# A wait behind one cast, and the order of the last stores, in a convolution with max pooling

## The chip, the core and the metric

The kernel runs on one core of one Trainium2 chip. The metric is the device time of one execution in microseconds (us): 105.42 us is the median of three runs before the change (105.28, 105.42 and 109.23). The core has five engines that each work through a queue of their own in order and wait for each other by semaphores: TensorE (PE, matmuls; PEld are its weight loads), VectorE (DVE), ScalarE (ACT), GpSimd (POOL), and SyncE (SP), which here only issues DMA transfers. Sixteen DMA engines move data between the device's memory and the on-chip memory.

## The reference

A 3x3 convolution without bias over 16 images of 64 channels and 64x64 pixels, to 128 channels, zero-padded by one pixel, then a 2x2 maximum without overlap. Input, weights and output are float32; the output is 16x128x32x32.

```python
x_pad = np.pad(x, ((0, 0), (0, 0), (pad, pad), (pad, pad)), mode='constant')
for b ...: for co ...: for ci ...: for kh ...: for kw ...:
    conv[b, co] += weight[co, ci, kh, kw] * x_pad[b, ci, kh:kh+h, kw:kw+w]
for b ...: for c ...: for i ...: for j ...:
    output[b, c, i, j] = np.max(conv[b, c, i*2:(i+1)*2, j*2:(j+1)*2])
```

## The kernel before

**Steps.** Two images are handled together: the 64 channels of the first lie on partitions 0 to 63, those of the second on 64 to 127. Each of the 8 pairs is cut into four quarters of 16 input rows, which gives 32 steps; a step makes 8 rows by 32 columns of pooled output for each of its two images. In the names, `24.1` is step 24 and its second image. An accumulator bank holds 8 rows by 64 columns of convolution for 128 output channels; there are eight banks.

**Two ways to compute a step.** Pooling needs two convolution rows at a time, y0 and y1, from four input rows x(-1), x0, x1, x2. With G0, G1, G2 the three kernel rows (each three taps, one matmul per tap, on 64 rows of partitions), a step of kind K takes the sum x0 + x1 (`KS`) on VectorE, multiplies it by G1 for both rows (`PR`), and makes two partial sums A (`PAa`, `PAb`) and B (`PBa`, `PBb`) from weights that are differences (D2 = G2 - G1, D0 = G0 - G1). A step of kind W makes S = x0 + x1, E = x0 - x1 and V, the differences of rows two apart, and has four products: `P2` (E), `P0` and `P3` (V), `P1` (S). In both the part common to y0 and y1 is added after the maximum of A and B.

**Around the products.** For each image of a step, ScalarE copies A out (`EV`) and, for kind W, copies A after `P2` into B's bank (`SE`, the seed); for some steps it also lifts a set of input rows into a bank (`CP`). VectorE takes the maximum of the two rows (`MX`). ScalarE copies the odd columns out (`OD`), and VectorE takes the maximum of even and odd columns into the output tile (`CM`). The very last image has its maximum over column pairs in one operation, in two halves (`RM`). `ST` stores a step's output tile of 256 KB; steps 30 and 31 are stored image by image (128 KB), the last image in halves of 64 KB, and the very last half is issued by ScalarE, all others by SyncE.

**Inputs.** W steps read float32 rows from the tiles `wx` (`LX`, issued by SyncE). K steps read bfloat16 rows from `kx`, which a GpSimd DMA casts on its way (`LK`), but for the first two K steps (0 and 2): these come as float32 into `kf` (`LX.0a`, `LX.0b`, `LX.2`) and are cast by an engine, `XO` for odd rows and `XE` for even ones. `XO.0a` (first half of step 0) is given to VectorE, the other four casts to ScalarE. A load waits (`paced`) for the column maxima of the step 12 or 13 places earlier.

**What sets the order.** The text ORDER is written out by hand as it stands: tokens in the order in which the program is recorded. Each engine gets its own tokens in that order, and nothing reorders them. A token on one engine does not hold back a token on another; only semaphores do, and they follow from the data, from the reuse of buffers and from one hand-made rule. A store thus waits for its step's `CM`, and whatever stands behind it on SyncE waits with it.

**The hand-made rule** is in `row_op` (line 194 is its operation): an element-wise row operation on GpSimd also waits for the last row operation that was recorded for VectorE before it, which `last_row` holds. VectorE's operations that read a bank beside the rows (line 288), its casts (line 189) and its work on banks are not held in it.

**The head around the change**, by engine, from the tokens: VectorE has V.1, TV.GP (line 240), XO.0a (line 189), TV.D0 and TV.G1 (line 242), E.3 and S.3 (line 288), then the row maxima of step 1. GpSimd has S.1, V.3, two casting loads (LK.5, LK.9), then S.4. TensorE has P0.1 for both images (its data named wv), then the first PAa of step 0 (kx), P3.1 (wv), more of step 0 (kx), P2.3 (we), again step 0, P1.1 (ws) and P0.3 (wv). ScalarE has SE.1, XO.0b and XE.0a, CP.3 (line 284), EV.1 twice, XE.0b and XE.2, EV.0 twice, SE.3 twice (line 421).

**The tail around the change**: behind the last load, SyncE's queue holds the stores of steps 21, 18, 22, 17, 15, 14, 16, 20, 26, 19, 23, 24, 28, 27, 25, 29, then 30.1, 30.0, 31.0 and the first half of 31.1.

Of the kernel before, what the change touches and what calls it, by code (L numbers as in the profile page):

```python
# [61 lines left out]
MX.22.0 P1.22.0 P3.24.1 CM.21.1 CM.20.1 LX.29 S.25:v SE.24.0:1 EV.24.1 OD.22.0 KS.27:v PAa.23.1:4  # L62
P2.25.0:2 E.26:g CM.22.0 ST.13 MX.24.1 P0.24.0 P2.25.1:7 SE.25.0:5 EV.24.0 PAb.23.1 P3.24.0 P0.25.0
PBa.23.1:6 MX.24.0 P1.24.1 PBa.23.0:0 KS.23:v EV.23.1 EV.25.0 SE.25.1:4 V.26:v LX.31 OD.24.1 S.26:g
LX.30 P1.24.0 PBb.23.1 OD.24.0 V.28:g E.29:g P3.25.0 P2.26.1:2 CM.24.1 ST.21 ST.18 SE.26.1:3 S.29:g
P0.25.1 PBb.23.0 CM.24.0 ST.22 ST.17 EV.25.1 P2.26.0:1 P3.25.1 SE.26.0:7 MX.25.0 MX.23.0 V.29:g
E.31:g P0.26.1 P1.25.0 MX.25.1 MX.23.1 OD.25.0 V.30:g ST.15 P3.26.1 PR.23.0 EV.26.1 OD.23.0 P0.26.0
P1.25.1 EV.26.0 CM.25.0 P3.26.0 PR.23.1 PAa.27.0:2 PAa.27.1:5 MX.26.1 CM.23.0 CP.28:1 ST.14 MX.26.0
OD.23.1 P1.26.1 PBa.27.0:0 OD.25.1 E.28:v CM.25.1 PAb.27.0 PAb.27.1 V.31:g PBb.27.0 P2.28.1:4
OD.26.1 ST.16 EV.27.0 CM.26.1 P1.26.0 PBa.27.1:3 CM.23.1 EV.27.1 P2.29.0:6 PBb.27.1 SE.28.1:2 S.28:v  # L70
OD.26.0 MX.27.0 CP.30:5 CM.26.0 PR.27.0 P0.28.1 SE.29.0:1 MX.27.1 OD.27.0 P3.28.1 P2.28.0:7 EV.28.1
E.30:v CM.27.0 P0.29.0 PR.27.1 SE.28.0:4 EV.29.0 OD.27.1 P3.29.0 P2.29.1:0 MX.28.1 ST.20 P1.28.1
P0.28.0 ST.26 ST.19 S.30:v ST.23 SE.29.1:6 P3.28.0 P2.30.1:5 MX.29.0 EV.28.0 OD.28.1 CM.27.1 P1.29.0
P0.29.1 SE.30.1:7 MX.28.0 S.31:g P2.30.0:3 P3.29.1 EV.29.1 CM.28.1 ST.24 P0.30.1 P1.28.0 OD.29.0
P3.30.1 P2.31.0:2 SE.30.0:0 EV.30.1 OD.28.0 CM.29.0 MX.29.1 MX.30.1 CM.28.0 P2.31.1:1 P0.30.0
SE.31.0:5 EV.30.0 P3.30.0 P1.29.1 P0.31.0 P1.30.1 SE.31.1:4 OD.29.1 MX.30.0 P0.31.1 P3.31.0 EV.31.0
CM.29.1 MX.31.0 EV.31.1 P3.31.1 P1.30.0 MX.31.1 P1.31.0 OD.30.1 OD.30.0 CM.30.1 ST.28 ST.27 ST.25
ST.29 ST.30.1 CM.30.0 ST.30.0 OD.31.0 P1.31.1 CM.31.0 RM.31.1a RM.31.1b ST.31.0 ST.31.1a ST.31.1b:a
"""


# [1 line left out]
def kernel(  # L83
# [98 lines left out]

    eng = {"v": nc.vector, "a": nc.scalar, "g": nc.gpsimd}

    def cast(e, out, in_):
        if e == "a":
            nc.scalar.copy(out=out, in_=in_)
        else:
            eng[e].tensor_copy(out=out, in_=in_)  # L189

    last_row = [None]

    def row_op(e, out, in0, in1, op):
        inst = eng[e].tensor_tensor(out=out, in0=in0, in1=in1, op=op)  # L194
# [5 lines left out]
    def weights(m, e):  # L200
        if m in ("g0", "g1", "g2"):
            cast(e, slots(m.upper()), {"g0": g0, "g1": g1, "g2": g2}[m])
        elif m == "D2":
            row_op(e, slots("D2"), g2, g1, SUB)
        elif m == "D0":
            row_op(e, slots("D0"), g0, g1, SUB)
        elif m == "GS":
            row_op(e, gsum, wv[:, 0:3, :], wv[:, 6:9, :], ADD)
        elif m == "GM":
            row_op(e, slots("GM"), ring(gsum, 0), g1, SUB)  # L210
        elif m == "GP":
            row_op(e, slots("GP"), ring(gsum, 0), g1, ADD)
# [58 lines left out]
    def to_bf16(s, part, odd, e):  # L271
        p, lo, hi = chunk(s)
        a, b = {"": (lo, hi), "a": (lo, half(s)), "b": (half(s), hi)}[part]
        a += (a % 2) != odd
        cast(e, kx_of(p)[:, a:b:2, :], kf[s][:, a - lo : b - lo : 2, :])
# [42 lines left out]
    def rs_cast(s, e):  # L318
        t = row["S", s] = row_pool.tile([128, R, W], BF16, name="ws")
        cast(e, t, wrow(s, 0))  # L320
# [263 lines left out]
```

## Time and profile before

| | |
|---|---|
| median of three runs | 105.42 us |
| the profiled execution | 104.88 us |
| its span, first to last instruction | 103.1 us |
| granted TensorE clock, mean | 0.998 |
| DMA over the span | 24.07 MB, 233 GB/s |

In the rows of a timeline the columns are the start in us from the beginning of the span, the length in us, the engine, the line, the operation, output and input by the program's names with partitions by elements and type, and how many instructions are merged (x2). In brackets stands how long the engine had been idle before, and what released it. Rows of a wait name the waiting engine and its line, then what it waited for: the total in us, how often, and the longest. Rows of DMA issues give the issuing queue, the size and the time from issue to landing. PEld rows are weight loads, which run ahead of the matmuls that use them. The ends of matmuls are modelled; their starts are what to go by.

### The profile page before, as it was taken

Reading aid. Unit: us, or ns where it says so; the run is one execution under the profiler, and the core shown is the slowest. Engines: PE = TensorE matmul, PEld = TensorE weight load, DVE = VectorE, ACT = ScalarE, POOL = GpSimd, SP = SyncE. Lnnn points to the kernel's source line nnn. Section 1 sums busy time; section 2 is a strip of 40 time slices with the busy share of each in tenths; the row PEclk is TensorE's granted clock in tenths of the full one; section 3 lists DMA queues with packets and bytes.
Section 4 is the critical chain, followed back from the end, with each engine's and each line's share of the span. In section 5 each row is a group of like instructions: output and inputs, shape, how many; then the busy total and the mean of one; then the engine's idle time right before and its main releaser. Section 6 shows DMA issues by size and latency. Waiting matters only on the chain.

```text
span 103.1 us, 2478 instructions
## 1 busy us (share of the span) xinstructions
PE 95.7 (93%) x870; PEld 51.9 (50%) x870; DVE 91.0 (88%) x176; ACT 89.4 (87%) x199; POOL 80.8 (78%) x63
## 2 busy tenths in 40 slices
PE   6696999999999999999999999999999999999920
PEld 2153754555555567565555575555444446455300
DVE  1599899999989999999999999778989999978860
ACT  4596999887989999998899999999998989999810
POOL 5006978999599969999998999999962999997000
PEclk9999999999999999999999999999999999999999
DMA  2989999839940699999999972898669700740881
GB/s 62 307 241 416 418 417 325 178 96 352 257 130 11 159 221 332 256 302 269 272 390 375 385 283 56 233 256 240 247 226 339 254 6 0 239 168 0 288 276 56
DMA packets 13789, 24.07 MB, mean 233 GB/s; under 512 B 1104, under 2 KB 9680, under 8 KB 13776
## 3 DMA queue, kind: packets, MB, share of 16 engines
q1 hardware_dynamic: 12768, 22.29, 64.5%
q0 software_dynamic: 864, 1.56, 8.5%
q8 instruction: 7, 0.11, 0.4%
q10 hardware_dynamic: 144, 0.07, 0.2%
q14 instruction: 6, 0.05, 0.2%
HBM read 17.07 MB, written 8.39 MB: 247 GB/s over the span
## 4 chain that ended last, share of the span: by engine, by line
PE 82%; DVE 7%; DMA 3%; ACT 3%; issue 1%; DVEq 0%; ACTq 0%
PE acc L393 82%; DMA wraw<-in_weight_dram 3%; DVE wq L194 2%; DVE kx L189 1%; ACT ev L408 1%; DVE wv L194 1%; DVE acc L425 1%; DVE we L194 1%; ACT od L448 1%; DVE gsum L194 0%; ACT acc L284 0%; ACT acc L421 0%; DVE o L457 0%; DVE wt L240 0%; DVEq L579 0%
## 5 line engine op out<-in xcount | busy, mean ns | idle before, releaser
L393 PEld LDWEIGHTS <-wt 64*128 64x128 bf16 x840 | 49.6, 94 | 41.4 <-issue 3.7
L393 PE MATMUL acc<-wv,wt 64*128 64x504 bf16 (+1 forms) x288 | 63.4, 377 | 0.5 <-DVE wt L240 0.5
L194 POOL TENSOR_TENSOR wv<-wx 128x1024 bf16<-128x1024 f32 x21 | 49.3, 2362 | 1.5 <-DMA wx<-in_x_dram 0.6
L425 DVE TENSOR_TENSOR acc<-acc,ev 128x512 f32<-128x512 f32 x64 | 43.6, 692 | 2.7 <-ACT ev L408 1.4
L393 PE MATMUL acc<-kx,wt 64*128 64x504 bf16 (+6 forms) x216 | 38.4, 350 | 0.4 <-DVE kx L189 0.4
L393 PE MATMUL acc<-we,wt 64*128 64x512 bf16 (+1 forms) x144 | 36.8, 376 | 0.1
L393 PE MATMUL acc<-ws,wt 64*128 64x512 bf16 (+1 forms) x144 | 35.0, 377 | 0.2 <-DVE acc L425 0.2
L408 ACT ACTIVATE ev<-acc 128x512 f32<-128x512 f32 x48 | 28.8, 605 | 1.5 <-PE acc L393 1.2
L421 ACT COPY acc<-acc 128x512 f32<-128x512 f32 x48 | 28.2, 591 | 1.3 <-DVE o L457 0.4
L457 DVE TENSOR_TENSOR o<-acc,od 128x256 f32<-128x256 f32 x63 | 25.0, 416 | 1.8 <-ACT od L448 1.3
L448 ACT COPY od<-acc 128x256 f32<-128x256 f32 x63 | 22.8, 379 | 1.6 <-PE acc L393 1.2
L194 POOL TENSOR_TENSOR ws<-wx 128x512 bf16<-128x512 f32 x12 | 15.2, 1273 | 9.6 <-DVE wv L194 6.2
L194 POOL TENSOR_TENSOR we<-wx 128x512 bf16<-128x512 f32 x10 | 12.7, 1272 | 2.0 <-DVE ks L194 1.2
L393 PE MATMUL acc<-ks,wt 64*128 64x504 bf16 (+1 forms) x48 | 12.9, 376 | 0.0
L410 ACT COPY ev<-acc 128x512 f32<-128x512 f32 x16 | 9.3, 595 | 1.0 <-PE acc L393 0.8
L288 DVE TENSOR_TENSOR we<-acc,wx 128x512 bf16<-128x512 f32 x11 | 7.5, 683 | 0.7 <-ACT acc L284 0.5
L288 DVE TENSOR_TENSOR ws<-acc,wx 128x512 bf16<-128x512 f32 x11 | 7.5, 679 | 0.0
L284 ACT COPY acc<-wx 128x512 f32<-128x512 f32 x11 | 6.7, 607 | 0.6 <-DMA wx<-in_x_dram 0.6
L485 PE MATMUL acc<-const-bfloat16-1.0 128*128 128x512 bf16 x8 | 3.3, 595 | 0.8 <-PEq L565 0.8
L194 DVE TENSOR_TENSOR ks<-kx 128x512 bf16<-128x512 bf16 x8 | 4.0, 511 | 0.0
L194 DVE TENSOR_TENSOR wv<-wx 128x1024 bf16<-128x1024 f32 x3 | 3.7, 1217 | 0.0
L269 POOL DMA_DIRECT2D kx<-in_x_dram x6 | 3.5, 586 | 0.0
(28 smaller groups left out, 23.0 us busy)
## 6 DMA issues: line engine op xcount, KB each, us to landing
out_dram<-o SPq DMA_DIRECT2D x30, 256.0 KB, 4.3
wx<-in_x_dram SPq DMA_DIRECT2D x12, 512.0 KB, 7.3
wx<-in_x_dram SPq DMA_DIRECT2D x6, 544.0 KB, 5.2
wx<-in_x_dram SPq DMA_DIRECT2D x6, 480.0 KB, 7.9
kx<-in_x_dram POOLq DMA_DIRECT2D x3, 256.0 KB, 7.8
kf<-in_x_dram SPq DMA_DIRECT2D x1, 512.0 KB, 8.2
kx<-in_x_dram POOLq DMA_DIRECT2D x2, 240.0 KB, 8.0
out_dram<-o SPq DMA_DIRECT2D x3, 128.0 KB, 2.9
```

Source lines behind the costliest of these rows:

```text
L194: inst = eng[e].tensor_tensor(out=out, in0=in0, in1=in1, op=op)
L269: paced(s, nc.gpsimd.dma_start(out=kx_of(p)[:, lo:hi, :], in_=rows_of(p, lo, hi)))
L284: nc.scalar.copy(out=acc[bank], in_=wrow(s, 0))
L288: nc.vector.tensor_tensor(out=t, in0=lifted[s], in1=wrow(s, 1), op=op)
L393: yield lambda kw=kw, o0=o0, o1=o1, c0=c0, c1=c1: nc.tensor.matmul(acc[t][:, i0:i1, o0:o1], wt[l * CI : l * CI + CI, K * BLOCKS[block] + T ...
L408: inst = nc.scalar.mul(t, acc[bank["A", s, l]], -1.0)
L410: inst = nc.scalar.copy(out=t, in_=acc[bank["A", s, l]])
L421: nc.scalar.copy(out=acc[b], in_=acc[bank["A", s, l]])
L425: nc.vector.tensor_tensor(out=t, in0=t, in1=ev[s, l], op=MAX)
L448: nc.scalar.copy(out=od[s, l][:, i0:i1], in_=acc[bank["B", s, l]][:, i0:i1, 1::2])
L457: done[s, l] = nc.vector.tensor_tensor(out=outs(s)[:, l, i0:i1], in0=acc[bank["B", s, l]][:, i0:i1, 0::2], in1=od[s, l][:, i0:i1], op=MAX,)
L485: nc.tensor.matmul(acc[n], ones[:, 0:128], ones, start=True, stop=True, skip_group_check=True)
```

## The change

First, `cast` records its operation in `last_row` when it runs on VectorE or GpSimd, so that GpSimd row operations recorded behind it wait for it too. Second, in the text ORDER the stores behind the last load (LX.30) are moved: each stands right behind the last `CM` of its step, those of steps already finished directly behind the load; ST.31.0 stands ahead of the last two `RM`. SyncE's queue behind the last load becomes 21, 18, 22, 17, 15, 14, 16, 20, 19, 24, 25, 23, 26, 27, 28, 29, 30.1, 30.0, 31.0 and the first half of 31.1. No instruction is added or taken away, and the queues of the other engines keep their order.

```diff
-LX.30 P1.24.0 PBb.23.1 OD.24.0 V.28:g E.29:g P3.25.0 P2.26.1:2 CM.24.1 ST.21 ST.18 SE.26.1:3 S.29:g
...
+LX.30 ST.21 ST.18 ST.22 ST.17 ST.15 ST.14 ST.16 ST.20 ST.19 P1.24.0 PBb.23.1 OD.24.0 V.28:g E.29:g
+P3.25.0 P2.26.1:2 CM.24.1 SE.26.1:3 S.29:g P0.25.1 PBb.23.0 CM.24.0 ST.24 EV.25.1 P2.26.0:1 P3.25.1
...
+MX.26.1 CM.23.0 CP.28:1 MX.26.0 OD.23.1 P1.26.1 PBa.27.0:0 OD.25.1 E.28:v CM.25.1 ST.25 PAb.27.0
+PAb.27.1 V.31:g PBb.27.0 P2.28.1:4 OD.26.1 EV.27.0 CM.26.1 P1.26.0 PBa.27.1:3 CM.23.1 ST.23 EV.27.1
+P2.29.0:6 PBb.27.1 SE.28.1:2 S.28:v OD.26.0 MX.27.0 CP.30:5 CM.26.0 ST.26 PR.27.0 P0.28.1 SE.29.0:1
...
+CM.27.1 ST.27 P1.29.0 P0.29.1 SE.30.1:7 MX.28.0 S.31:g P2.30.0:3 P3.29.1 EV.29.1 CM.28.1 P0.30.1
+P1.28.0 OD.29.0 P3.30.1 P2.31.0:2 SE.30.0:0 EV.30.1 OD.28.0 CM.29.0 MX.29.1 MX.30.1 CM.28.0 ST.28
...
+P0.31.1 P3.31.0 EV.31.0 CM.29.1 ST.29 MX.31.0 EV.31.1 P3.31.1 P1.30.0 MX.31.1 P1.31.0 OD.30.1
+OD.30.0 CM.30.1 ST.30.1 CM.30.0 ST.30.0 OD.31.0 P1.31.1 CM.31.0 ST.31.0 RM.31.1a ST.31.1a RM.31.1b
+ST.31.1b:a

+    last_row = [None]
+
     def cast(e, out, in_):
         if e == "a":
             nc.scalar.copy(out=out, in_=in_)
         else:
-            eng[e].tensor_copy(out=out, in_=in_)
-
-    last_row = [None]
+            last_row[0] = eng[e].tensor_copy(out=out, in_=in_)
```

More of the change, by code (lines that the diff above doesn't have):

```diff
@@ L64 @@
 PBa.23.1:6 MX.24.0 P1.24.1 PBa.23.0:0 KS.23:v EV.23.1 EV.25.0 SE.25.1:4 V.26:v LX.31 OD.24.1 S.26:g
-LX.30 P1.24.0 PBb.23.1 OD.24.0 V.28:g E.29:g P3.25.0 P2.26.1:2 CM.24.1 ST.21 ST.18 SE.26.1:3 S.29:g
-P0.25.1 PBb.23.0 CM.24.0 ST.22 ST.17 EV.25.1 P2.26.0:1 P3.25.1 SE.26.0:7 MX.25.0 MX.23.0 V.29:g
-E.31:g P0.26.1 P1.25.0 MX.25.1 MX.23.1 OD.25.0 V.30:g ST.15 P3.26.1 PR.23.0 EV.26.1 OD.23.0 P0.26.0
-P1.25.1 EV.26.0 CM.25.0 P3.26.0 PR.23.1 PAa.27.0:2 PAa.27.1:5 MX.26.1 CM.23.0 CP.28:1 ST.14 MX.26.0
@@ L69 @@
[L69 to L78, printed above, removed]
+LX.30 ST.21 ST.18 ST.22 ST.17 ST.15 ST.14 ST.16 ST.20 ST.19 P1.24.0 PBb.23.1 OD.24.0 V.28:g E.29:g
+P3.25.0 P2.26.1:2 CM.24.1 SE.26.1:3 S.29:g P0.25.1 PBb.23.0 CM.24.0 ST.24 EV.25.1 P2.26.0:1 P3.25.1
@@ new lines @@
+SE.26.0:7 MX.25.0 MX.23.0 V.29:g E.31:g P0.26.1 P1.25.0 MX.25.1 MX.23.1 OD.25.0 V.30:g P3.26.1
+PR.23.0 EV.26.1 OD.23.0 P0.26.0 P1.25.1 EV.26.0 CM.25.0 P3.26.0 PR.23.1 PAa.27.0:2 PAa.27.1:5
+MX.26.1 CM.23.0 CP.28:1 MX.26.0 OD.23.1 P1.26.1 PBa.27.0:0 OD.25.1 E.28:v CM.25.1 ST.25 PAb.27.0
+PAb.27.1 V.31:g PBb.27.0 P2.28.1:4 OD.26.1 EV.27.0 CM.26.1 P1.26.0 PBa.27.1:3 CM.23.1 ST.23 EV.27.1
+P2.29.0:6 PBb.27.1 SE.28.1:2 S.28:v OD.26.0 MX.27.0 CP.30:5 CM.26.0 ST.26 PR.27.0 P0.28.1 SE.29.0:1
+MX.27.1 OD.27.0 P3.28.1 P2.28.0:7 EV.28.1 E.30:v CM.27.0 P0.29.0 PR.27.1 SE.28.0:4 EV.29.0 OD.27.1
@@ new lines @@
+P3.29.0 P2.29.1:0 MX.28.1 P1.28.1 P0.28.0 S.30:v SE.29.1:6 P3.28.0 P2.30.1:5 MX.29.0 EV.28.0 OD.28.1
+CM.27.1 ST.27 P1.29.0 P0.29.1 SE.30.1:7 MX.28.0 S.31:g P2.30.0:3 P3.29.1 EV.29.1 CM.28.1 P0.30.1
+P1.28.0 OD.29.0 P3.30.1 P2.31.0:2 SE.30.0:0 EV.30.1 OD.28.0 CM.29.0 MX.29.1 MX.30.1 CM.28.0 ST.28
+P2.31.1:1 P0.30.0 SE.31.0:5 EV.30.0 P3.30.0 P1.29.1 P0.31.0 P1.30.1 SE.31.1:4 OD.29.1 MX.30.0
+P0.31.1 P3.31.0 EV.31.0 CM.29.1 ST.29 MX.31.0 EV.31.1 P3.31.1 P1.30.0 MX.31.1 P1.31.0 OD.30.1
+OD.30.0 CM.30.1 ST.30.1 CM.30.0 ST.30.0 OD.31.0 P1.31.1 CM.31.0 ST.31.0 RM.31.1a ST.31.1a RM.31.1b
```

## The prediction

> **What bounds the kernel now.** First the page's busy times and the chain that ended last, then the pieces of that chain in order of time (start, length, what).
>
> ```profile
> PE 95.7 (93%) x870; PEld 51.9 (50%) x870; DVE 91.0 (88%) x176; ACT 89.4 (87%) x199; POOL 80.8 (78%) x63
> ...
> PE 82%; DVE 7%; DMA 3%; ACT 3%; issue 1%; DVEq 0%; ACTq 0%
> ```
>
> ```profile
> 9.65 35.60 PE acc L393 x346
> ...
> 47.85 48.56 PE acc L393 x442
> ...
> 99.28 0.33 DVE o L467
> ```
>
> From 9.65 to 96.4 us TensorE runs from matmul to matmul, but for 2.6 us around 45 to 48. Four engines are near full, so a gain at one place lasts only if no other engine sets the pace right behind it. The two edits touch the two ends: the head before 9.65 us, and the last stores.
>
> **Part 1, the wait.** In the order, the one cast given to VectorE is XO.0a; the next GpSimd operations behind it are S.1 and V.3, and S.1, being first, carries the wait. No other GpSimd operation is affected: the next row operation of VectorE (KS.0) takes over as what is waited for. The timeline of the head, by engine:
>
> ```profile
> 8.37 1.23 DVE L189 CAST kx<-kf 128x256 bf16<-128x256 f32 x1
> 9.52 0.61 DVE L242 COPY wt<-acc 128x384 bf16<-128x384 bf16 x2
> ```
>
> ```profile
> 8.19 1.26 POOL L194 TENSOR_TENSOR ws<-wx 128x512 bf16<-128x512 f32 x1 [6.22 <-DVE wv L194]
> 10.02 2.37 POOL L194 TENSOR_TENSOR wv<-wx 128x1024 bf16<-128x1024 f32 x1 [0.56 <-DMA wx<-in_x_dram]
> ```
>
> ```profile
> 8.46 0.82 PE L393 MATMUL acc<-wv,wt 64*128 64x512 bf16 x6 [0.49 <-DVE wt L240]
> 9.65 0.51 PE L393 MATMUL acc<-kx,wt 64*128 64x256 bf16 x6 [0.37 <-DVE kx L189]
> ...
> 13.50 0.82 PE L393 MATMUL acc<-ws,wt 64*128 64x512 bf16 x6
> 14.15 1.14 PE L393 MATMUL acc<-wv,wt 64*128 64x512 bf16 x7
> ```
>
> The cast begins 0.18 us into S.1 (8.19 to 9.45) and ends at 9.60, 0.15 us after it: it looks held by S.1. TensorE waits for it. What the cast takes alone is not in the trace. Below, 0.15 us, what was left of it behind S.1; above, 1.23 us, if it is slow by itself. The nearest row of its size is this one of VectorE:
>
> ```profile
> L457 DVE TENSOR_TENSOR o<-acc,od 128x256 f32<-128x256 f32 x63 | 25.0, 416 | 1.8 <-ACT od L448 1.3
> ```
>
> I take 0.3 us, under those 416 ns. Then the cast ends at 8.67. TensorE is free at 8.46 + 0.65 = 9.11 (six such matmuls take 0.65 from start to start, 13.50 to 14.15), so it starts its cast rows at 9.11 and not at 9.65: 0.54 us earlier. At 1.23 us nothing is won here.
>
> The Trainium skill, "SBUF — State Buffer", section "SBUF: two separate sides", has a rule for this: a VectorE operation in a two-port mode and a GpSimd operation exclude each other, and the later one is blocked until the first has ended. By that rule the cast is short alone; the two rows above agree (0.15 us behind the end at 9.45). By it the sum of this part would be as I take it, 0.54 us at TensorE's start.
>
> The added wait costs GpSimd: S.1 starts at 8.67 + 0.09 (the handover seen before it, from wv's end at 8.10 to 8.19) = 8.76 and ends at 10.02, 0.57 later. Behind it in the queue stands V.3, which sat 0.56 us idle for its load until 10.02 anyway, so the load hides it. With the upper bound S.1 runs from 9.69 to 10.95, V.3 ends at 13.32 in place of 12.39, and its reader, the wv matmuls at 14.15, still does not wait. Lost on GpSimd: nothing in both cases. The two copies of VectorE behind the cast come earlier, beside S.1; held by it they would start near 10.0, 0.5 us later than now, and end at 10.6, before VectorE's next work, which waits for ScalarE.
>
> What is late next? ScalarE, whose rows behind the head are these, and with them TensorE's weight loads:
>
> ```profile
> 10.05 0.59 ACT L284 COPY acc<-wx 128x512 f32<-128x512 f32 x1 [0.56 <-DMA wx<-in_x_dram]
> 10.58 1.08 ACT L408 ACTIVATE ev<-acc 128x512 f32<-128x512 f32 x2
> 11.54 0.93 ACT L187 CAST kx<-kf 128x256 bf16<-128x256 f32 x2
> 12.36 1.08 ACT L410 COPY ev<-acc 128x512 f32<-128x512 f32 x2
> 13.31 1.10 ACT L421 COPY acc<-acc 128x512 f32<-128x512 f32 x2
> ```
>
> ```profile
> 13.98 0.10 PEld L393 LDWEIGHTS <-wt 64*128 64x128 bf16 x2 [0.15 <-ACT acc L421]
> 14.46 0.54 PEld L393 LDWEIGHTS <-wt 64*128 64x128 bf16 x7 [0.39 <-issue]
> ```
>
> ScalarE is released at 10.02 by a load that the change does not touch, and from 10.05 to 14.41 it has no gap. Its last two copies, the seeds of step 3 (SE.3.0 to 13.90, SE.3.1 to 14.41), release TensorE's P0.3 products: the weight loads resume at 13.98 and 14.46, 0.05 to 0.08 us behind each copy. TensorE coming 0.54 us earlier stands there and waits. So I count the head's 0.54 us as lost again by 14.46: sum of part 1, **0.0 us**; the ends are 0 and 0.54 won.
>
> **Part 2, the stores.** SyncE issues in order, and a store waits for its step's column maximum on VectorE. No load moves: the order up to LX.30 is kept, and the eight stores behind it are the same in both (21, 18, 22, 17, 15, 14, 16, 20), so the loads' company is as before. SyncE's issues and its wait, before (of the last row's eight, the first is ST.28, then 27, 25, 29 and the four that hold steps 30 and 31):
>
> ```profile
> 79.04 0.71 SPq L480 DMA_DIRECT2D out_dram<-o  x1
> ```
>
> ```profile
> SPq L480 <- DVE o L457: 7.7, 1, 7.7
> ```
>
> ```profile
> 87.48 1.97 SPq L480 DMA_DIRECT2D out_dram<-o  x4
> ```
>
> ```profile
> 94.87 5.09 SPq L480 DMA_DIRECT2D out_dram<-o  x8
> ```
>
> After the store at 79.04 (ST.20), ST.26 blocks the queue for 7.7 us; ST.19, 23 and 24, long done, stand behind it. Then ST.28 blocks ST.27 and ST.25 until 94.87. The stretches of 2 us show the cost (last two columns: DMA share, GB/s):
>
> ```profile
> 84.00:86.00 2.00, 2.00 (x23) 1.15 (x19) 1.99 (x5) 1.57 (x5) 2.00 (x2) 1.00 0.00 0
> ...
> 92.00:94.00 2.00, 2.00 (x22) 1.06 (x19) 1.45 (x4) 2.00 (x6) 2.00 (x2) 1.00 0.00 0
> ...
> 96.00:98.00 2.00, 1.77 (x14) 0.63 (x11) 1.76 (x4) 1.44 (x4) 0.00 (x0) 1.00 1.04 341
> 98.00:100.00 2.00, 0.66 (x4) 0.09 (x1) 1.54 (x5) 0.37 (x1) 0.00 (x0) 1.00 0.83 278
> ```
>
> The DMA engines idle and are then full for the last 4 us. After the change ST.19 goes out behind ST.20, and 24, 25, 23, 26, 27 each at its step, so of the group at 94.87 only ST.28 and ST.29 are left before the last ones: 512 KB fewer. No waiter on VectorE's buffers shows in the stretch; earlier stores only free them earlier. ST.26 goes from first to fifth of these, and still has over 10 us to the end.
>
> The end of the span is the landing of the last store, issued on ScalarE's queue:
>
> ```profile
> 99.64 0.37 ACTq L480 DMA_DIRECT2D out_dram<-o  x1
> ```
>
> ```profile
> out_dram<-o ACTq DMA_DIRECT2D x1, 64.0 KB, 2.5
> ```
>
> ```profile
> out_dram<-o SPq DMA_DIRECT2D x1, 256.0 KB, 2.2
> ```
>
> The first landing is that store's; the second is that of the store issued at 87.48, when the engines were idle. 99.64 + 2.5 = 102.14, and 0.96 us later the span ends. Its issue hangs on TensorE, ScalarE and VectorE (the chain's last piece ends at 99.61) and does not move. Its landing can come nearer: four times the bytes took 2.2 us on idle engines. Upper bound 2.2; lower bound 2.2 less 192 KB at 341 GB/s (0.58) = 1.6. I take **1.9**, the middle: 0.6 us won, ends 0.3 and 0.9.
>
> Why more than bytes may be won: code is fetched over the same engines. Queues, packets, MB and share of 16 engines from 95 to 99.5 us:
>
> ```profile
> q1 hardware_dynamic: 1197, 1.15, 77.3%
> q8 instruction: 1, 0.02, 1.2%
> q14 instruction: 1, 0.01, 0.4%
> ```
>
> One packet of 1.2% is 0.012 x 16 x 4.5 = 0.86 us of a single engine, the other 0.29; stores take 3.48 us of each. Should one engine get both, it has 4.63 us of work in 4.5 and runs late to the end; a store has landed only when its slowest engine is done. Without 0.52 of the 1.15 MB it has 3.05 us and catches up.
>
> The Trainium skill, "DMA: Bandwidth & Descriptors", section "Anatomy of one DMA — SWDGE (gpsimd) path", gives a transfer a fixed 2.0 us and bytes at 436 GB/s, written for another issuing path. By it (an estimate) 64 KB land in 2.15 us, and the part wins 0.35 us; it speaks against more. The 2.2 us for 256 KB are under the 2.6 it gives, so the trace leaves room below.
>
> **Sum.** 0.0 + 0.6 = 0.6 us. The profiled execution took 104.88 us with a span of 103.1, so 104.28 after. It lies 0.54 under the median of 105.42, so against the timed runs I expect 105.42 - 0.6 = **104.8**.
>
> **Rivals.** *Head gain survives:* if ScalarE runs ahead of TensorE between 14.5 and 45 us, 0.54 us stays. Against it stand the two weight loads that resume right behind ScalarE. 105.42 - 0.54 - 0.6 = 104.3.
>
> *Nothing lands earlier:* the last stores are held by their own latency or by the late engine, which the code fetch alone makes late. For it: the last 64 KB need 2.5 us although DMA was at 0.83 by then. 105.4.
>
> *Slower:* the new wait ties GpSimd to the load of kf. Place: S.1, then V.3, then TensorE's P0.3. Price: V.3 must end by 14.4, so start by 12.0, so the cast must end by 10.7 (S.1 takes 1.26 and the handover 0.09). Beyond that point each us of lateness costs one. The cast ended by 8.67 needs a load that is 2 us late to reach that point. Against it: the cast's load had landed before 8.37. With up to 1.1 us beyond the point it would give 105.4 to 106.5.
>
> *The change does not do what it says:* no edit moves TensorE, ScalarE or VectorE in their order, and on SyncE the last four stores stay where they were; should they alone decide, it is the second rival.
>
> **How the numbers follow.** Forecast 0.53, head gain too 0.13, nothing 0.24, slower 0.10. The range reaches from 103.9 (0.54 and 0.9 won) to 105.9 (nothing won, and half of the slower case). 2% are 2.1 us, about what a measurement of this kernel can tell from no change; every case but a strong form of the third rival lies inside. Faster by over 2%: 0.04; within: 0.90; slower: 0.06.
>
> **What would show it.** The cast's row near 0.3 us at 8.4, S.1 from about 8.8, TensorE's kx matmuls at 9.1, the weight load at 14.46 unmoved. DMA at work between 80 and 92 us without the two empty stretches; a group of two, not four, 256 KB stores from 94.87; the last store's landing near 1.9 us. I am wrong if matmuls behind 14.46 come 0.3 us earlier or later than now, or if the last landing stays over 2.3.

## The result and the profile after

The changed kernel takes 104.05 us (median of six runs, 103.8 to 104.35), the kernel before beside it 105.35 us. The ratio is 0.9893, with a 95% interval of 0.9868 to 0.9919: 1.13 us less (0.85 to 1.39). The forecast was 0.6 us: direction and range held, the size was half. Of the 124 runs of kernels without the wait 9 took over 106.5 us (the 109.23 is one), of the 89 with it none; the ratios leave such runs out, and why they come is not shown here. The profiled execution fell by 0.88 us, from 104.88 to 104.0 us (span 103.1 to 102.2), so the two traces account for less than the timed runs.

*The head.* VectorE, GpSimd, TensorE and ScalarE of the changed kernel, one after the other (start, length, engine, line, operation):

```profile
8.54 0.28 DVE L192 CAST kx<-kf 128x256 bf16<-128x256 f32 x1
8.74 0.62 DVE L243 COPY wt<-acc 128x384 bf16<-128x384 bf16 x2
```

```profile
8.91 1.27 POOL L195 TENSOR_TENSOR ws<-wx 128x512 bf16<-128x512 f32 x1 [6.95 <-DVE kx L192]
10.14 2.36 POOL L195 TENSOR_TENSOR wv<-wx 128x1024 bf16<-128x1024 f32 x1
```

```profile
8.64 0.82 PE L394 MATMUL acc<-wv,wt 64*128 64x512 bf16 x6 [0.49 <-DVE wt L241]
9.28 0.51 PE L394 MATMUL acc<-kx,wt 64*128 64x256 bf16 x6
...
13.82 1.13 PE L394 MATMUL acc<-wv,wt 64*128 64x512 bf16 x7
```

```profile
9.72 0.59 ACT L285 COPY acc<-wx 128x512 f32<-128x512 f32 x1 [0.46 <-DMA wx<-in_x_dram]
...
12.98 1.10 ACT L422 COPY acc<-acc 128x512 f32<-128x512 f32 x2
```

```profile
13.64 0.10 PEld L394 LDWEIGHTS <-wt 64*128 64x128 bf16 x2 [0.16 <-ACT acc L422]
14.12 1.82 PEld L394 LDWEIGHTS <-wt 64*128 64x128 bf16 x18 [0.39 <-issue]
```

The cast takes 0.28 us where it took 1.23, S.1 starts behind it, and TensorE goes from wv to kx without the stop of 0.37 us. Here the whole head began 0.18 us later (wv at 8.64, before 8.46), because step 1's load landed later (at 5.90 us, before 5.72). The two weight loads of P0.3 come at 13.64 and 14.12, 0.34 us earlier than before (13.98 and 14.46), and that shift holds: between 20 and 92 us matmul after matmul starts 0.32 to 0.34 us earlier. But ScalarE's lift of step 3's rows (line 285, before line 284) also starts 0.33 us earlier, 9.72 for 10.05, and it was released by a load that the change does not touch. So this pair of traces alone cannot say whether the 0.33 us are the change's.

*The tail.* SyncE's waits for landings at the very end (1.1 us in three waits, before 1.8 in six), the last store's landing, and four stretches of 2 us (last two columns: DMA share and GB/s):

```profile
SPq L580 <- DMA out_dram<-o: 1.1, 3, 0.4
```

```profile
out_dram<-o ACTq DMA_DIRECT2D x1, 64.0 KB, 2.0
```

```profile
84.00:86.00 2.00, 2.00 (x22) 1.29 (x20) 1.99 (x6) 1.57 (x5) 2.00 (x2) 1.00 0.25 87
...
92.00:94.00 2.00, 2.00 (x22) 1.11 (x20) 1.53 (x3) 2.00 (x6) 2.00 (x2) 1.00 0.26 87
...
96.00:98.00 2.00, 1.77 (x14) 0.50 (x8) 1.81 (x4) 1.34 (x4) 0.00 (x0) 1.00 0.53 173
98.00:100.00 2.00, 0.34 (x2) 0.00 (x0) 1.23 (x4) 0.17 (x1) 0.00 (x0) 0.86 0.57 187
```

DMA works in the two stretches that were empty (0.25 and 0.26 for 0.00), and the last two are at 0.53 and 0.57 where they were at 1.04 and 0.83. The last store lands 1.96 us behind its issue (99.32 to 101.28 in the trace's completions; before 99.64 to 102.15, 2.51 us). That is 0.55 us of the 0.88; the other 0.33 are the head's.

### The profile page after: what moved, and what is told of

It is laid out like the page before. It is cut to its first block, busy times and chain, and to the rows that moved or that the text cites. A ratio compares the mean times of both kernels' runs of the same rounds, so it can differ in the third digit from the quotient of the medians.

```text
span 102.2 us, 2482 instructions
## 1 busy us (share of the span) xinstructions
PE 95.7 (94%) x870; PEld 52.2 (51%) x870; DVE 90.1 (88%) x176; ACT 89.3 (87%) x199; POOL 80.8 (79%) x63
## 4 chain that ended last, share of the span: by engine, by line
PE 84%; DMA 5%; DVE 4%; ACT 3%; issue 1%; SPq 0%; DVEq 0%; ACTq 0%
PE acc L394 84%; DMA wx<-in_x_dram 5%; ACT ev L409 1%; DVE wv L195 1%; DVE acc L426 1%; DVE we L195 1%; ACT od L449 1%; DVE wq L195 1%; ACT acc L285 0%; ACT acc L422 0%; DVE o L458 0%; DVE wt L241 0%; SPq L519 0%; DVE o L468 0%; DVEq L580 0%
```

## The experiments

The questions: are the head's 0.33 us the change's doing, or the luck of a load? And is the tail's gain what stands ahead of the last stores, as the prediction had it? All ratios are against the kernel before on the same chip, each with its 95% interval; four kernels at a time shared a chip. Theory A is the prediction's (the wait wins nothing), theory B that it wins what the load of step 3 allows.

**The halves alone.** First only the cast's edit, then only the new order of the stores.

```diff
-            eng[e].tensor_copy(out=out, in_=in_)
+            last_row[0] = eng[e].tensor_copy(out=out, in_=in_)
```

> Only the wait behind the cast; the stores stand as before. Theory A (the prediction's): ScalarE holds TensorE at step 3's seeds whatever TensorE does before, so 0.0 us, ratio 0.999 to 1.001. Theory B: the head's gain is kept as far as the load of step 3 lets ScalarE come early, so 0.3 us (0.2 to 0.5), ratio near 0.997. In the profile both have the cast near 0.3 us and TensorE's kx matmuls 0.65 us behind the wv matmuls; they part at the second weight load of P0.3 (14.46 before, 14.12 after).

Measured: 0.9995 (0.997 to 1.002), 0.05 us. TensorE and ScalarE of this run:

```profile
8.46 0.82 PE L393 MATMUL acc<-wv,wt 64*128 64x512 bf16 x6 [0.49 <-DVE wt L240]
9.11 0.51 PE L393 MATMUL acc<-kx,wt 64*128 64x256 bf16 x6
...
14.29 0.70 PE L393 MATMUL acc<-wv,wt 64*128 64x512 bf16 x3
```

```profile
10.19 0.59 ACT L284 COPY acc<-wx 128x512 f32<-128x512 f32 x1 [0.57 <-DMA wx<-in_x_dram]
```

The kx matmuls start at 9.11, just as worked out, 0.54 us earlier than before; and P0.3 starts at 14.29, 0.14 later than before. The lift came 0.14 later too (10.19 for 10.05). The whole 0.54 us are lost behind the lift, as theory A has it.

```diff
-... OD.30.0 CM.30.1 ST.28 ST.27 ST.25
-ST.29 ST.30.1 CM.30.0 ST.30.0 OD.31.0 P1.31.1 CM.31.0 RM.31.1a RM.31.1b ST.31.0 ST.31.1a ST.31.1b:a
+(the order of the changed kernel, with the cast as before)
```

> Only the order of the stores; no wait behind the cast. Theory A: all of the change's gain, 1.1 us, ratio 0.989, and a last landing more than 1 us earlier in most runs. Theory B: the tail's part alone, 0.55 us (the last landing 2.0 us behind its issue where it was 2.5), ratio near 0.995.

Measured: 0.9936 (0.9913 to 0.996), 0.67 us (0.42 to 0.92). That is theory B's 0.55 within its interval, not theory A's 1.1. So each theory was right of one half, and the two halves made 0.72 us of the 1.13; with intervals of about 0.26 us to each side, these two do not differ clear of noise.

**Is ScalarE the pace in the head?** One of its casts (even rows of step 2) goes from ahead of step 0's copies to behind step 3's seeds, with and without the wait behind VectorE's cast.

```diff
-... PBb.0.0a PBb.0.1a LX.6 XE.2:a
+... PBb.0.0a PBb.0.1a LX.6
...
-... MX.0.1 P0.3.0 P0.3.1 XO.2:a MX.0.0 ...
+... MX.0.1 P0.3.0 P0.3.1 XE.2:a XO.2:a MX.0.0 ...
```

> The changed kernel, with one cast of ScalarE (even rows of step 2) moved from ahead of step 0's copies to behind step 3's seeds: 0.46 us less on ScalarE ahead of the seeds. If ScalarE sets the pace there (both theories say so of the changed kernel), the second weight load of P0.3 comes 0.3 us nearer to TensorE's kx start, and the time falls by 0.2 to 0.35 us against the changed kernel (103.75). If TensorE's own chain sets it, nothing changes (104.05).

> The same move of ScalarE's cast, with the stores' new order and without the wait behind the cast: now the held cast of VectorE sets the pace. If the two bounds are about equal in the kernel before, this wins less than with the wait, 0 to 0.15 us against the stores alone; TensorE's P0.3 then starts near 14.15 in any case.

Measured: 0.9923 (0.9899 to 0.9947) with the wait, 104.36 us, and 0.9943 (0.9923 to 0.9963) without, 104.51 us. The expected 103.75 did not come, and the ratio is no lower than those of the changed kernel itself (0.9893, and 0.9923 and 0.9909 below), which did not run beside them. Without the wait, P0.3 started at 14.14 as expected, and the time was that of the stores alone (104.57). ScalarE, with the wait:

```profile
10.40 0.59 ACT L285 COPY acc<-wx 128x512 f32<-128x512 f32 x1 [0.60 <-DMA wx<-in_x_dram]
...
13.45 1.06 ACT L422 COPY acc<-acc 128x512 f32<-128x512 f32 x2
14.41 0.63 ACT L190 CAST kx<-kf 128x512 bf16<-128x512 f32 x1
```

The second seed ends 4.11 us behind the start of the lift (10.40 to 14.51), where it was 4.36 (10.05 to 14.41): 0.25 us won there. But the moved cast then stands in front of step 1's copies on the same engine, which start 5.05 us behind the lift (before 4.77), and from 20 us on the matmuls are 0.46 us later than before with a lift 0.35 us later, so the 0.25 are more than given back. ScalarE has hardly a gap there; moving work within it moves the place of the wait. Without the wait, the lift's row names another releaser:

```profile
9.90 0.59 ACT L285 COPY acc<-wx 128x512 f32<-128x512 f32 x1 [0.78 <-DVE wt L243]
```

The load had landed (at 9.43), and ScalarE waited for VectorE's copy out of the bank into which it lifts. That copy (TV.D0) stands behind the held cast. So the cast that GpSimd holds also holds ScalarE. The prediction had seen only TensorE wait for it.

**The changed kernel again, and the tail's group.** The repeat is unchanged; the other puts two stores back behind ST.28.

> The changed kernel once more, beside the kernel before on one chip. If the part of the change's 1.1 us that the two halves alone do not show (0.05 and 0.67 us, 0.72 in sum) was chance in which load landed early, the ratio comes out near 0.993; if the two halves help each other, it stays near 0.989. In the profile the shift of the middle (matmuls from 20 to 95 us) equals the shift of ScalarE's lift of step 3's rows, to 0.05 us, whichever way that load landed.

Measured: 0.9923 (0.989 to 0.9957), 0.81 us. The lift started at 9.75, 0.30 earlier than before, and the middle was 0.30 earlier. The first 1.13 us were at the upper end, and the expected 0.993 for chance came.

```diff
-... CM.25.1 ST.25 ...
+... CM.25.1 ...
-CM.27.1 ST.27 ...
+CM.27.1 ...
-... CM.28.0 ST.28
+... CM.28.0 ST.28 ST.27 ST.25
```

> The changed kernel with two stores put back: steps 27 and 25 go behind step 28 again, so the group in front of the last stores is again of four (1 MB), while all others keep their new place. If the 512 KB in front of the last stores are what the tail's gain is, it is gone: last landing near 2.5 us behind its issue, ratio near 0.999 (with the wait's effect 0). If the earlier drain between 80 and 92 us is what counts, the gain stays near 0.993.

Measured: 0.9954 (0.9927 to 0.9982), and the last store's landing (and with it the queues from 94.7 to 99.2 us):

```profile
out_dram<-o ACTq DMA_DIRECT2D x1, 64.0 KB, 2.7
```

```profile
q1 hardware_dynamic: 1182, 1.13, 76.9%
q8 instruction: 1, 0.02, 1.3%
q14 instruction: 1, 0.01, 0.8%
```

The same queues of the changed kernel in the same stretch:

```profile
q1 hardware_dynamic: 692, 0.66, 44.2%
q8 instruction: 1, 0.02, 1.2%
```

And SyncE's waits for landings at the end, with the two stores put back:

```profile
SPq L580 <- DMA out_dram<-o: 1.9, 6, 0.6
```

With 512 KB back in front, the landing goes from 1.95 us (the repeat) to 2.69 behind the issue, though all other stores keep their early places: the earlier drain between 80 and 92 us does not by itself bring the last landing nearer. All traces agree: with the group of four, ScalarE's store lands 2.43 to 2.92 us behind its issue (before, cast alone twice, and this one), in the ten others 1.93 to 1.98. The timed runs alone do not part this kernel from the repeat (0.9954 and 0.9923, with intervals that overlap). The last store's 16 completions show how: 15 come from 101.08 to 101.33, one at 102.06. In the kernel before, the last is 0.57 us behind the other 15 (102.15 for 101.58); in the changed kernel all 16 lie between 101.08 and 101.28, though step 29's store, issued a good 3 us before the last one, still has a straggler (99.33 for 98.11). It looks as if one DMA engine falls behind by over 1 us and, in the changed kernel, has caught up when the last store comes. That a code packet makes it late fits the times (packets of 0.88 to 0.96 us at 96.9 to 97.4 us in these three traces), but the traces do not name the engine. One rival stays open: queue 14's code packet of 8 KB starts 0.6 to 1.4 us ahead of the last store's issue in the four traces with the group of four, and 6.7 to 6.8 us ahead of it in the ten others. It moves with the stores, so no run parts its share from that of the 512 KB. The ratio of 0.9954 is lower than the 0.999 expected: in its trace the middle is 0.27 us earlier, which alone would make 0.9974, inside the interval.

**Step 3's load first.** One place earlier on SyncE, with ScalarE's cast that used the other load put behind the lift.

```diff
-... TV.D2:a LX.0b LX.3 P2.1.0:5 ...
+... TV.D2:a LX.3 LX.0b P2.1.0:5 ...
-... TV.GP:v XO.0b:a XO.0a:v ...
+... TV.GP:v XO.0a:v ...
-P3.1.1 TV.D0:v LX.8 XE.0a:a CP.3:1 PAa.0.1b ...
+P3.1.1 TV.D0:v LX.8 XE.0a:a CP.3:1 XO.0b:a PAa.0.1b ...
```

> The changed kernel with the load of step 3 issued one place earlier (ahead of the second half of step 0's first rows) and ScalarE's cast of that half put behind the lift of step 3's rows. If that load sets the pace through ScalarE once the cast is not held, the lift starts 0.3 to 0.6 us earlier, and the middle with it: 0.3 us under the changed kernel. If TensorE's chain from the cast sets it, no gain.

> The same, without the wait behind the cast (stores in the new order). Here the held cast keeps TensorE's kx matmuls near 9.65, so the earlier load can win little: 0.0 to 0.1 us against the stores alone, and 0.2 to 0.4 us slower than the same with the wait. That difference is what the wait is worth where the load is early.

Measured: with the wait 0.9893 (0.9852 to 0.9934), without it 0.9912 (0.9883 to 0.9942). The lift's row, with the wait and without:

```profile
9.12 0.59 ACT L285 COPY acc<-wx 128x512 f32<-128x512 f32 x1 [0.17 <-DVE wt L243]
```

```profile
10.56 0.59 ACT L285 COPY acc<-wx 128x512 f32<-128x512 f32 x1 [1.11 <-DVE wt L243]
```

With the load out of the way, both lifts wait for VectorE's copy: with the wait 0.58 us behind the cast's start (8.54), without it 1.54 us behind it (9.02). The traces differ by 1.15 us in the middle, 0.48 of it because that second run's cast also began that much later; the timed runs differ by 0.19% (0.2 us), which their intervals do not tell from nothing.

**All on one chip.** Cast alone, stores alone, both, and both with step 3's load first.

> The wait alone once more, now on one chip with the other three. The profiles so far say: what the wait wins is the smaller of 0.54 us and what the landing of step 3's load allows behind the held copies. So between 0 (load near 10.1 to 10.4 us) and 0.35 us (load near 9.7): ratio 0.9965 to 1.000. In the profile: middle shifted as the lift of step 3's rows is.

> The stores alone once more. The tail is worth 0.5 to 0.6 us on any chip: ratio 0.9945; the last landing 1.9 to 2.0 us behind its issue.

> Both. The sum of the two above, to within 0.3 us: the halves touch the two ends and do not help each other. If they do help each other, this is over 0.3 us better than the sum.

> Both, with step 3's load first. If the head is held by that load, 0.0 to 0.4 us better than both alone, more where the wait alone wins little; ratio 0.988 to 0.991.

| | ratio | 95% interval | us |
|---|---|---|---|
| cast alone | 0.9975 | 0.9953 to 0.9996 | 0.26 |
| stores alone | 0.9927 | 0.9898 to 0.9956 | 0.77 |
| both | 0.9909 | 0.9878 to 0.9941 | 0.96 |
| both, step 3's load first | 0.9911 | 0.9871 to 0.9952 | 0.93 |

The us are the ratio's distance from one times 105.05. The sum of the halves is 1.03, both give 0.96: they touch two ends and add up, within the intervals. Whether step 3's load first is better than the change as it is stays unclear: 0.9893 beside 0.9923 on the chip of the repeat, 0.9911 beside 0.9909 here. Its twelve runs here spread from 103.59 to 105.56 us, and the median of all of them, 104.72, is only 0.33 us under 105.05. The last store's landing, stores alone and then cast alone (where SyncE's half lands last, 2.61 us behind its issue):

```profile
out_dram<-o ACTq DMA_DIRECT2D x1, 64.0 KB, 2.0
```

```profile
out_dram<-o ACTq DMA_DIRECT2D x1, 64.0 KB, 2.4
```

Last, the bounds of the head. Cast alone, and then both, on this chip (TensorE's kx and P0.3, ScalarE's lift):

```profile
9.49 0.51 PE L393 MATMUL acc<-kx,wt 64*128 64x256 bf16 x6
...
14.00 1.03 PE L393 MATMUL acc<-wv,wt 64*128 64x512 bf16 x7
```

```profile
9.52 0.59 ACT L284 COPY acc<-wx 128x512 f32<-128x512 f32 x1
```

```profile
9.09 0.51 PE L394 MATMUL acc<-kx,wt 64*128 64x256 bf16 x6
...
13.75 1.13 PE L394 MATMUL acc<-wv,wt 64*128 64x512 bf16 x7
```

```profile
9.65 0.59 ACT L285 COPY acc<-wx 128x512 f32<-128x512 f32 x1 [0.57 <-DMA wx<-in_x_dram]
```

In the first, P0.3 starts 4.51 us behind kx and 4.48 behind the lift; in the second, 4.66 and 4.10. In eight traces (before, after, the repeat, the tail of four, cast alone twice, and stores alone and both on this chip), P0.3 starts to within 0.02 us at the later of two times: kx plus 4.50, lift plus 4.10. Before: 9.65 + 4.50 = 14.15 and 10.05 + 4.10 = 14.15, the row says 14.15. After: 13.78 and 13.82, the row says 13.82. Cast alone, first: 13.61 and 14.29; 14.29. Cast alone, here: 13.99 and 13.62; 14.00. The repeat of the change: 13.52 and 13.85; 13.85. In the kernel before, both bounds met to 0.01 us. That is P0.3's first image. The weights of its second came at 14.46, right behind the second seed and 0.31 us behind the first image's matmul; in cast alone, here, at 14.06, 0.06 behind it. So ScalarE did hold TensorE there before, by about 0.25 us.

The shift that lasts is set further on, by a path that the prediction does not have. E.3 and S.3 wait for the lift, E.4 stands behind them on VectorE, S.4 on GpSimd waits for E.4 by the hand-made rule, V.4 follows it, and P0.4 on TensorE reads V.4. S.4, V.4 and P0.4 before, and then cast alone on this chip:

```profile
14.18 1.27 POOL L194 TENSOR_TENSOR ws<-wx 128x512 bf16<-128x512 f32 x1 [0.62 <-DVE we L194]
15.41 2.36 POOL L194 TENSOR_TENSOR wv<-wx 128x1024 bf16<-128x1024 f32 x1
...
17.82 0.37 PE L393 MATMUL acc<-wv,wt 64*128 64x512 bf16 x1
```

```profile
13.90 1.29 POOL L194 TENSOR_TENSOR ws<-wx 128x512 bf16<-128x512 f32 x1
15.14 2.36 POOL L194 TENSOR_TENSOR wv<-wx 128x1024 bf16<-128x1024 f32 x1
...
17.56 0.37 PE L393 MATMUL acc<-wv,wt 64*128 64x512 bf16 x1
```

In ten of the fourteen traces, before and after among them, S.4 starts 4.12 to 4.13 us behind the lift. In the three in which the lift came earliest for the cast (cast alone here, and step 3's load first with the wait, twice), S.4 stands instead 4.78 to 4.79 us behind S.1, with no wait: there GpSimd's own queue sets the pace, and S.1 is late because it waits for the cast. P0.4 starts 3.64 to 3.66 us behind S.4 in ten traces, 0.05 to 0.06 us behind V.4's end, and in these the middle is shifted as P0.4 is, to 0.02 us. In cast alone, here, P0.3's second image is 0.40 us earlier than before, P0.4 and the middle only 0.26 to 0.27, with a lift 0.53 us earlier; the expected shift as the lift's did not come.

From this an estimate of what the wait wins in one execution. Without the wait, the lift starts no earlier than 1.54 us behind the cast's start (9.90 for 8.36, 10.56 for 9.02), so S.4 no earlier than 5.67 behind it. With the wait, S.1 starts 0.37 behind the cast's start, so S.4 no earlier than 5.15: at most 0.52 us can be won. In the traces with the wait and the loads in their old order, S.4 is earlier than that 5.67 by 0.37 us (after), 0.07 (repeat), 0.21 (tail of four), 0.25 (both, here) and 0.52 (cast alone, here); in the first of cast alone, and with ScalarE's cast moved, the load came too late, and nothing is won. So the head's 0.33 us were the change's and the load's together: the load landed earlier, and in that head the held cast would have kept the lift until 10.08.

## Why the prediction was right and wrong

**Part 1, the cast.** Right: 0.3 us alone (0.28), held by S.1, kx 0.65 us behind wv (0.64), S.1 from about 8.8 (8.91), V.3 only 0.12 us later (10.14 for 10.02) and in time for its reader. The two copies behind the cast ran beside S.1 and were not held by it (0.62 us, before 0.61). In one more trace without the wait (stores alone, first) the cast began at 10.11, beside V.3 (9.98 to 12.32), and took 2.36 us, to 12.47, again 0.15 us behind the end of GpSimd's operation. The Trainium skill's rule, "SBUF — State Buffer", section "SBUF: two separate sides", that one of the two engines blocks the other for a whole instruction, agrees with the cast's 1.23 and 2.36 us beside GpSimd and 0.28 us alone. Not quite right was "Lost on GpSimd: nothing": in three traces S.1's later start set S.4, and with it P0.4.

**Part 1, what is late next.** This is the step that failed, as a term of the sum: "I count the head's 0.54 us as lost again by 14.46: sum of part 1, 0.0 us". P0.3 does wait for ScalarE's seeds, and these for the lift, as written; the shift that lasts hangs on the same lift by VectorE and GpSimd (S.4, V.4, P0.4), a path that the prediction left out. Either way the sum stands on the lift, and its start was read from one execution, in which its load released GpSimd and ScalarE at 10.02 and 10.05. In the traces with the wait in which the load released it, the lift started from 9.65 to 10.40; in one (cast alone, second) at 9.52 with no wait for it. And the zero left out that the held cast bars ScalarE as well, through the bank that VectorE's copy frees. In the rows of before, that second bound lay just ahead of the load: the two copies behind the cast run from 9.52 to 10.13, so the first ends near 9.83, and a lift whose load had landed started at 9.90 with the cast at the same time (8.36; the row in the experiment on ScalarE), 0.15 us ahead of 10.05. Where the load is late, the wait wins nothing (lift at 10.19 in the first trace of cast alone); where it is early, the kernel before still stands behind the cast, and the wait wins up to 0.52 us by the estimate above. Timed, the term put at 0.0 was 0.05 and 0.26 us. In single traces of the whole change the middle is up to 0.41 us earlier (both, on the last chip). I had put 0.13 on the rival that the whole 0.54 us stay; what happened lies between.

**Part 2, the stores.** Right in mechanism and nearly in size: 0.6 us forecast, 0.67 and 0.77 measured for the stores alone, 0.55 between the traces of before and after (1.9 us to landing forecast, 1.96 measured); over all traces the nearer landing is worth 0.45 to 0.99 us. The group of four in front and the one late completion of 16 were seen. That the late one is the engine that fetches code, and how much of the gain is the 512 KB and how much the second code packet, is not shown. The rival that nothing lands earlier is out. The estimate by the Trainium skill, "DMA: Bandwidth & Descriptors", section "Anatomy of one DMA — SWDGE (gpsimd) path", 2.15 us for 64 KB, was 0.2 us too long for this issuing path: the trace has 1.96.

**The slower rival** did not come: the cast alone is not slower in either measurement, and V.3 was not late for TensorE in any of its traces.

**The sum.** 0.0 + 0.6 stood for 0.0 to 0.3 + 0.7. Three measurements of the whole change gave 1.13, 0.81 and 0.96 us, with intervals that overlap; the forecast of 0.6 is 0.53, 0.74 and 0.62 of them. (The lower end of the range is 103.98 by its own terms, not 103.9.) That the first was the largest is, as far as the runs show, chance. What stays open is when that load lands in the timed runs, of which one for each kernel has a trace: the share of the wait between 0 and 0.5 us cannot be assigned to the others.

## What to carry to other kernels

A gain counted as "lost to the next engine" should be worked out from the times of both bounds, and from what each bound would be if its releaser came earlier: here the next engine hung on the same held instruction through a buffer, 0.15 us ahead of a load that varies by more than that. It pays to follow the released work on until a shift lasts: here two steps further, over two other engines. In this kernel, stores that waited behind an unfinished step cost nothing until the last ones; what counted is what is still queued, or fetched beside it, when the last small store is issued, since it is done only with the last of its 16 completions.

## What was not expected

The landing of one and the same 512 KB load moves from execution to execution: issued at 2.58 or 2.59 us, it was complete between 9.41 and 10.30 us in the eleven traces with the same order of loads, which is more than the effect in question. And a store's completions can be spread by over 1 us: 15 within 0.25 us of each other, and one far behind (98.11 and 99.33 us for step 29's store).
